# Host layouts, an earlier h and woven tables in the first mixer of a hybrid trunk

## The chip, the cores and the metric

The kernel runs on one core of a Trainium2 chip. Its time is in device microseconds (us), the median of several executions. A profiled execution stands beside it; its span is the time from the first to the last instruction. Engines are named as in the profile: PE (matmuls and transposes), DVE, ACT, POOL (elementwise work) and SP (here a queue that only issues transfers).

## The reference

Two layers over 256 latent tokens and 256 context tokens of width 1024. Layer 0 mixes with a long convolution ("Hyena") on 768 channels beside a state space model ("S5") on 256; layer 1 mixes with a gated linear recurrence; each is followed by a mixture of experts (MoE). The change concerns what leads up to the mixer of layer 0.

```python
def rmsnorm(x, g):
    x32 = x.astype(F32)
    y = x32 * lax.rsqrt(jnp.mean(x32 * x32, axis=-1, keepdims=True) + EPS)
    return (y * g).astype(x.dtype)
...
def s5_discretise(lam_re, lam_im, log_step, b_re, b_im):
    lam = lax.complex(lam_re.astype(F32), lam_im.astype(F32))
    dt = jnp.exp(log_step.astype(F32))[..., None]
    lam_bar = jnp.exp(lam * dt)
    b_bar = ((lam_bar - 1.0) / lam)[..., None] * lax.complex(b_re.astype(F32), b_im.astype(F32))
    return lam_bar, b_bar
...
    p_lat = h_lat @ w_in
    u_lat = s5_in(p_lat)
    st_lf = s5_scan(u_lat, lam_bar[0], b_bar[0], st_cf[:, -1], False)
...
        y = jnp.concatenate([hyena_mix(p[..., :3 * HY_D], filt, conv_w, conv_b, hy_bias),
                             s5_readout(u, st_f, st_b, c_mat, d, glu_w, glu_b)], axis=-1)
        return y.astype(p.dtype) @ w_out
```

Here h is the normed input, scaled and shifted per channel by values made from a conditioning vector (the "modulation"); `w_in` projects it to 2304 channels for the convolution and 256 for the state space.

## The kernel before

`layer0_mixer` works in stages. `boot` loads x and ctx as tokens by channels (`x_sb`), transposes them on PE into `xT` (channels by tokens), squares and sums them (`sq`, `ssq`), makes the reciprocal root (`rs`, spread over partitions by `dg`), and multiplies (`nm`). Four modulation tiles `mod(0)` to `mod(3)`, 8 matmuls of a 2 MB weight tile each with 4 transposes behind them, give scale and shift; `modulate(0)` and `modulate(1)` turn halves of `nm` into h. h is kept as a high part `h_0` (ACT) and a remainder `h_1`: DVE computes scale and shift once more, then subtracts the high part.

Between these steps `boot` works off small generators: `s5_powers` (powers and phasors of the state space, `pw`, `ph`; the phasors on POOL through `tE`, `tF`, `tG`, `st`), `s5_inout` (tables `wB`, `C`, from `brow` and `crow` by transposes), `filter_net` (a two-layer net of the convolution's filters, `hdn`, `kf`, `r`).

A projection block (class `Channels`) is 128 output channels. Its weights are split into a high part `whi` (ACT) and a remainder `wlo` (POOL; for the very first block DVE); 24 matmuls of 512 columns follow, three for each of 8 slices of h (`mm3`: whi on h_0, whi on h_1, wlo on h_0). Blocks and further modulation tiles (`Mods`) form a list `fill`, and `drive(main, fill)` writes a main generator's work with as much fill between its steps as the step names for a gap. The order within each engine is fixed when the program is built.

The main generators after `boot` are `s5_mixer`, `s5_glu` (its matmuls read `gw`) and the convolutions. `s5_mixer` first runs the two blocks for its own channels (`uT`), then four quarters. A quarter is: `U,Gm` matmuls, copies `pq` on ACT, a chain of about 8 us on DVE (`tA`, `rot`, `sc`, `prev`), beside it small matmuls `Hm,wB` and `C,wB` whose result `KX` is spread by 8 transfers into `Km`, and at the end matmuls on `Km` and `prev`. Quarters meet the next through `Gm`; a transpose chain (`y`, `YT`) ends them. A convolution unit runs `zv` matmuls, DVE products, `yy` matmuls and again, six units in all.

2 MB weight tiles come through a ring of three buffers (`Feed.load`, on SP, in order); a tile is loaded when the one in its buffer has been read for the last time.

Of the kernel before, what the change touches and what calls it, by code (L numbers as in the profile page):

```python
# [237 lines left out]
def boot(E, o, feed, hT, hdn2):  # L238

    a, V, SY = E.a, E.V, E.SY
    pers = E.pers
    spec = [
        ('c', a['c'].rearrange("o (k p) -> (o k) p", p=P)),
        ('cc', a['c_ctx'].rearrange("(k p) -> k p", p=P)),
        ('n1', a['norm1_g'].rearrange("l (k p) -> (l k) p", p=P)),
        ('mb', a['mod_b'].rearrange("l (k p) -> (l k) p", p=P)),
        ('cw', a['hy_conv_w'].rearrange("o w (k p) -> (o w k) p", p=P)),
        ('cb', a['hy_conv_b'].rearrange("o (k p) -> (o k) p", p=P)),  # L250
        ('hb', a['hy_bias'].rearrange("o r (k p) -> (o r k) p", p=P)),
        ('glb', a['s5_glu_b'].rearrange("o (k p) -> (o k) p", p=P)),
        ('n2', a['norm2_g'].rearrange("l (k p) -> (l k) p", p=P)),
        ('cg', a['c_norm_g'].rearrange("o (k p) -> (o k) p", p=P)),
        ('lb', a['c_lower_bounds'].rearrange("d l (k p) -> (d l k) p", p=P)),
    ]
# [25 lines left out]
    def rows(gi):  # L282
        rt = bp.tile([P, P], F32, name=f"rows{gi}")
        for nm, ap, r0, r in groups[gi]:
            SY.dma_start(rt[r0:r0 + r, :], ap)
            E.prm[nm] = pt[:, gi, r0:r0 + r]
        return rt[:r0 + r], gi

    def columns(rt, gi):
        n = rt.shape[0]  # L290
        b = E.bank("s5")
        E.tr(b[:, :n], rt)
        E.copy(pt[:, gi, :n], b[:, :n])
# [3 lines left out]
    r0 = rows(0)
    x_sb = bp.tile([P, 4, D], F32, tag="x", name="x_sb")
    SY.dma_start(x_sb[:, 0:2, :], a['x'][0].rearrange("(j p) d -> p j d", p=P))
    SY.dma_start(x_sb[:, 2:4, :], a['ctx'][0].rearrange("(j p) d -> p j d", p=P))  # L300
    pows = s5_powers(E, o, E.tp)
    next(pows)
    feed.load()
    flt = filter_net(E, hdn2, bp)
    next(flt)
    feed.load()
    inout = s5_inout(E, o, E.tp)
    next(inout)
    feed.load()

    columns(*r0)
# [5 lines left out]
    late = []  # L317

    def sums(k, sq):
        for j in range(4):  # L320
            E.mm(ssq[32 * j:32 * j + 32, :n4], E.ones[:, :32], sq[:, j * n4:(j + 1) * n4], k == 0, k == KD - 1)

    def mod(q):
        with E.first():
            cols = mod_tile(E, 0, q, feed.ready['m', 0, q], later=True)
        feed.load()

        def finish():
            with E.first():
                cols()  # L330
        return finish
# [16 lines left out]
    with E.tc.manual_schedule(engines={E.TE.engine, E.S.engine}):
        for k in range(KD):
            b = E.bank("s5")  # L350
            for j in range(4):
                E.tr(b[:, j * P:(j + 1) * P], x_sb[:, j, k * P:(k + 1) * P])
            sq = E.mod.tile([P, 512], F32, tag="ms", name="sq", bufs=2)
            if k % 2:
                E.copy(E.xT[:, k, :], b)
            else:
                E.act(E.xT[:, k, :], b, AF.Copy)
            E.act(sq, b, AF.Square)
            late.append((k, sq))
            if k:  # L360
                sums(*late.pop(0))
            steps(pows, 3)
        sums(*late.pop())
# [1 line left out]
        mean_sq(E, ssq, 4, D)
        for _ in rms_g(E, 4, E.bank("s5")):
            steps(pows, 1)
        steps(inout, 1)
        rb = spread(E, 4, bp, "dg", E.bank("s5"))
        cols()  # L370
        nm = bp.tile([P, KD, T], F32, tag="x", name="nm")
        for k in range(KD):
            E.tt(nm[:, k], E.xT[:, k], rb, MUL)
            steps(pows, 2)
        cols = mod(1)
        steps(flt, 2)
        run(pows)
        cols()
        steps(flt, 7)
        cols = mod(2)  # L380
        later = [rows(q) for q in range(1, len(groups))]
        run(flt)
        cols()
        steps(inout, 2)
        with E.first():
            modulate(0)
        cols = mod(3)
        cols()
        wux = feed.ready['ux']
        ws = [split_w(E, wux[:, :, m * P:m * P + P], 0, KD, E.G if m else E.V) for m in range(2)]  # L390
        with E.first():
            modulate(1)
        run(inout)
        T0 = s5_quarter_tables(E, o, 0, E.hp, E.tq)
        next(T0)
        for x in later:
            columns(*x)
    return T0, ws

# [159 lines left out]
def filter_net(E, hdn2, fl):  # L559

    a, SY = E.a, E.SY
    zt = fl.tile([33, 256], F32, name="zt")
    SY.dma_start(zt, a['k_z'])
    fw1 = fl.tile([33, 64], F32, name="fw1")
    SY.dma_start(fw1, a['hy_fw1'][0])
    fw2 = fl.tile([64, 64], F32, name="fw2")
    SY.dma_start(fw2, a['hy_fw2'][0])
    fr = fl.tile([4, 64], F32, name="fr")
    for i, nm in enumerate(('hy_fb1', 'hy_ff1', 'hy_fb2', 'hy_ff2')):
        SY.dma_start(fr[i:i + 1, :], a[nm])  # L570
    yield
    b = E.bank("s5")
    E.tr(b[:64, :4], fr)
    fp = fl.tile([64, 4], F32, name="fp")
    E.copy(fp, b[:64, :4])
    yield
    cur = zt
# [104 lines left out]
def s5_powers(E, o, tp):  # L682
# [16 lines left out]
    yield  # L699
    E.copy(r4[:, 2], bcast(lst, 2, 64))  # L700
    b = E.bank("s5")
    for i in range(3):
        E.tr(b[:, i * 16:(i + 1) * 16], rows[:, i, :])
    lam = tp.tile([P, 3, 16], F32, name="lam")
    E.copy(lam.rearrange("p i g -> p (i g)"), b[:, :48])
# [1487 lines left out]
```

## Time and profile before

| | us |
|---|---|
| median of 3 runs (1487.02 to 1487.53) | 1487.36 |
| profiled execution | 1486.51 |
| its span | 1484.7 |
| PE busy | 1285.4 |
| DVE busy | 809.5 |
| POOL busy | 400.0 |
| ACT busy | 387.5 |

The mean granted clock of TensorE is 0.932 of full speed. What lies outside the span is 1.8 us. Layer 0's mixer takes about the first 530 us.

### The profile page before, as it was taken

What the parts mean: (1) busy time and instruction counts of PE and PEld (TensorE: products, weight loads), DVE (VectorE), ACT (ScalarE), POOL (GpSimd) and SP (SyncE); (2) the same over time, 40 slices, a digit from 0 to 9 for tenths busy, and PEclk for the clock granted to TensorE, in tenths of its full rate; (3) what the DMA queues carried; (4) which work ended last, traced back from release to release, by engine and by line L of the source; (5) the groups of instructions that cost most, each with busy time, mean ns of one, the idle gap of its engine ahead of it and who ended that gap; (6) DMA issues with size and microseconds to landing.
All of it is one profiled execution on the core that took longest, in us unless ns stands there. A gap on an engine that the chain in (4) does not pass through costs nothing. (4 is left out here: it accounts for less than half of the span.)

```text
span 1484.7 us, 18755 instructions
## 1 busy us (share of the span) xinstructions
PE 1285.4 (87%) x7093; PEld 826.7 (56%) x7093; DVE 809.5 (55%) x1785; ACT 387.5 (26%) x655; POOL 400.0 (27%) x326
## 2 busy tenths in 40 slices
PE   6499999898886769999999498979798969999995
PEld 4266766575665443444444277878778733444443
DVE  5856554766666453344335685665656553343443
ACT  2233433132232321111111443333333312121211
POOL 2733431334554321111100452323231221111101
PEclk9699999899988779999999698999999979999998
DMA  8415673145121389999994111211213189999970
GB/s 298 181 57 183 225 259 142 57 144 218 42 91 79 117 340 416 393 388 384 383 385 175 43 62 53 78 64 59 84 60 122 65 339 395 418 419 420 419 314 31
DMA packets 55747, 311.91 MB, mean 210 GB/s; under 512 B 14441, under 2 KB 19994, under 8 KB 24282
## 3 DMA queue, kind: packets, MB, share of 16 engines
q1 hardware_dynamic: 50746, 303.72, 52.2%
q0 software_dynamic: 4608, 6.30, 1.3%
q8 instruction: 61, 1.00, 0.3%
q10 hardware_dynamic: 288, 0.52, 0.1%
q14 instruction: 44, 0.36, 0.1%
HBM read 315.76 MB, written 4.19 MB: 215 GB/s over the span
## 5 line engine op out<-in xcount | busy, mean ns | idle before, releaser
L148 PE MATMUL pg_t<-w,Xe 128*64 128x512 f32 x1024 | 228.7, 599 | 0.0
L148 PE MATMUL in_t<-h,whl 128*128 128x512 f32 (+1 forms) x768 | 147.2, 349 | 3.2 <-DVE h L158 2.4
L148 PEld LDWEIGHTS pg_t<-w,Xe 128*64 128x64 f32 x1024 | 71.1, 138 | 135.7 <-issue 131.1
L161 POOL TENSOR_TENSOR whl<-wraw,whl 128x2048 fp32r<-128x2048 f32 x20 | 93.6, 4684 | 175.6 <-ACT whl L155 175.6
L148 PEld LDWEIGHTS in_t<-h,whl 128*128 128x128 f32 x768 | 121.7, 195 | 22.1 <-POOL h L161 3.1
L148 PE MATMUL py_t<-w,hid 128*64 128x512 f32 x512 | 119.1, 606 | 4.2 <-DVE yl L161 3.0
L164 DVE SCALAR_TENSOR_TENSOR sg<-sg,ws,pg_t 128x256 f32<-128x256 f32 x32 | 15.4, 480 | 180.2 <-ACT sg L155 180.2
L1615 POOL MEMSET Xg<- 128x1024 f32 x32 | 30.4, 959 | 295.6 <-PE ga_t L152 295.6
L164 DVE SCALAR_TENSOR_TENSOR xT<-sc_t,mT,xT 128x256 f32<-128x256 f32 x204 | 90.3, 479 | 29.6 <-PE sc_t L148 28.1
L161 POOL TENSOR_TENSOR wlo<-w,whi 128x1024 fp32r<-128x1024 f32 (+3 forms) x51 | 72.0, 1416 | 107.6 <-ACT whi L155 100.7
L148 PE MATMUL sc_t<-OT,yh 128*128 128x512 f32 (+1 forms) x256 | 90.7, 369 | 10.2 <-DVE xT L164 7.6
L148 PE MATMUL in_t<-h,whi 128*128 128x512 f32 x288 | 97.6, 416 | 2.1 <-ACT ms L155 1.4
L148 PE MATMUL sc_t<-OT,yl 128*128 128x512 f32 (+1 forms) x256 | 82.6, 337 | 0.0
L148 PEld LDWEIGHTS sc_t<-OT,yh 128*128 128x128 f32 x256 | 48.0, 188 | 54.2 <-issue 27.9
L148 PEld LDWEIGHTS py_t<-w,hid 128*64 128x64 f32 x512 | 34.1, 138 | 64.8 <-issue 55.9
L155 ACT ACTIVATE yh<-py_t 128x1024 fp32r<-128x1024 f32 (+1 forms) x34 | 33.1, 974 | 121.5 <-PE py_t L148 117.3
L168 DVE TENSOR_SCALAR OT<-ht_t,ksq 128x512 fp32r<-128x512 f32 (+1 forms) x32 | 19.7, 616 | 81.5 <-PE ht_t L148 81.5
L155 ACT ACTIVATE sg<-pg_t 128x256 f32<-128x256 f32 x32 | 12.3, 385 | 195.3 <-PE pg_t L148 195.2
L148 PEld LDWEIGHTS in_t<-h,whi 128*128 128x128 f32 x288 | 51.5, 190 | 17.9 <-issue 5.2
L148 PE MATMUL at_t<-QA,X 128*128 128x128 f32 x224 | 37.5, 318 | 26.9 <-DVE QA L161 26.9
L1670 POOL DMA_INDIRECT Xg<-rows,ix x32 | 32.3, 1010 | 104.9 <-DVE ws L1676 33.4
L148 PE MATMUL in_t<-whl,h 128*128 128x256 f32 x384 | 56.5, 300 | 3.7 <-POOL whl L161 3.7
(442 smaller groups left out, 2446.1 us busy)
## 6 DMA issues: line engine op xcount, KB each, us to landing
w<-in_w_gu_dram SPq DMA_DIRECT2D x128, 1024.0 KB
w<-in_w_dn_dram SPq DMA_DIRECT2D x64, 1024.0 KB
w<-in_w_mod_dram SPq DMA_DIRECT2D x24, 2048.0 KB
wraw<-in_w_in_dram SPq DMA_DIRECT2D x20, 1024.0 KB
w<-in_w_in_dram SPq DMA_DIRECT2D x5, 2048.0 KB
w<-in_w_out_dram SPq DMA_DIRECT2D x2, 2048.0 KB
cwo<-in_w_out_dram SPq DMA_DIRECT2D x2, 2048.0 KB
rows<-hh SPq DMA_DIRECT2D x6, 512.0 KB
```

What stands on the lines that cost most here:

```text
L148: self.TE.matmul(o, l, r, start=st, stop=sp)
L155: self.S.activation(o, i, f, **k)
L161: (e or self.V).tensor_tensor(o, x, y, op=op)
L164: self.V.scalar_tensor_tensor(o, x, s, y, op0=op0, op1=op1)
L168: (e or self.V).tensor_scalar(o, x, s1, None, op0=op0)
L1615: E.G.memset(X, 0.0)
L1670: E.G.indirect_dma_start(X, None, rows, bass.IndirectOffsetOnAxis(ix[:, pi:pi + 1], 0), bounds_check=n - 1, oob_is_err=False)
```

## The change

The host lays out x transposed, all parameter vectors as columns, and the state space's lam, B, C and D as the tables want them: the transposes in `boot` and most of its small transfers go. `boot` keeps only the norm, the modulation tiles (in the order 0, 2, 1, 3, so that the first half of h needs two of them) and `modulate`, in which ACT now scales and shifts in place, DVE casts the high part, and DVE and POOL subtract by turns. The tables become a main generator `tables`, driven with fill, and their phasors move from POOL to DVE. The two blocks for `uT` become `Inputs` at the head of the fill; the order of blocks changes from 2 `x2`, 4 `vx4`, 4 `x2` to 2 `Inputs`, 6 `x2`, 4 `vx4`. The transfers into `Km` are issued by ACT and not by SP.

```diff
+    SY.dma_start(pt, a['params'])
+    for k in range(0, KD, 2):
+        SY.dma_start(E.xT[:, k:k + 2], a['xT'][:, k:k + 2])
...
-                E.act(hT[0][:, k, sl], t[:, sl], AF.Identity, scale=A[:, r, k:k + 1], bias=mT[:, r, k:k + 1])
-                E.ts(t[:, sl], t[:, sl], A[:, r, k:k + 1], MUL, mT[:, r, k:k + 1], ADD)
-            E.tt(hT[1][:, k], t, hT[0][:, k].bitcast(F32), SUB, E.G if k % 4 == 1 else E.V)
+                E.act(t[:, sl], t[:, sl], AF.Identity, scale=A[:, r, k:k + 1], bias=mT[:, r, k:k + 1])
+            E.copy(hT[0][:, k], t)
+            E.tt(hT[1][:, k], t, hT[0][:, k].bitcast(F32), SUB, E.G if k % 2 else E.V)
...
-        cmul(E, (st[:, 0], st[:, 1]), (ph[:, 0, :, h], ph[:, 1, :, h]), (ph[:, 0, :, h], ph[:, 1, :, h]), (tG[:, 0], tG[:, 1]), G)
-        cmul(E, (ph[:, 0, :, n:2 * n], ph[:, 1, :, n:2 * n]), (ph[:, 0, :, 0:n], ph[:, 1, :, 0:n]),
-             (bcast(st[:, 0], 2, n), bcast(st[:, 1], 2, n)), (tE[:, :, :n], tF[:, :, :n]), G)
+        yield from cmul_g(E, (st[:, 0], st[:, 1]), (ph[:, 0, :, h], ph[:, 1, :, h]), (ph[:, 0, :, h], ph[:, 1, :, h]), (tG[:, 0], tG[:, 1]))
+        yield from cmul_g(E, (ph[:, 0, :, n:2 * n], ph[:, 1, :, n:2 * n]), (ph[:, 0, :, 0:n], ph[:, 1, :, 0:n]),
+             (bcast(st[:, 0], 2, n), bcast(st[:, 1], 2, n)), (tE[:, :, :n], tF[:, :, :n]))
...
-        E.SY.dma_start(Km[16 * i:16 * i + 16], KX[:, :, (7 - i) * 16:(7 - i) * 16 + P])
+        E.S.dma_start(Km[16 * i:16 * i + 16], KX[:, :, (7 - i) * 16:(7 - i) * 16 + P])
...
+class Inputs(Channels):
+
+
+    def after(self):
+        self.E.act(self.y(), self.b, AF.Copy)
...
-        for q in range(4):
+        for q in (0, 2, 1, 3):
             mw(0, q)
...
+        for m in range(2):
+            jobs.append(Inputs(E, feed, 'ux', m * P, 0, hT, lambda m=m: o.uT[:, m]))
         x2('ux', 256, 4)
         x2('ux', 384, 5, True)
+        block('x2')
+        for u in range(4):
+            x2('x2', u * P, u, u == 3)
         block('vx4')
         vx('vx4', 4)
         vx('vx4', 5)
-        block('x2')
-        for u in range(4):
-            x2('x2', u * P, u, u == 3)
-            mod()
+        mod(4)
...
+        def tables():
+            for _ in weave(s5_powers(E, o, tp), filter_net(E, o.net, hdn2, tp)):
+                yield 0.5
+            for _ in s5_inout(E, o, tp):
+                yield 1.0
+            next(tabs)
+            yield 2.0
+
+        drive(tables(), fill)
```

What ACT does from the first modulation tile to the first weight split was, in the program before (`ms` evacuates a modulation tile, `h_0_87` is the high part of h, each x8 is one half of it):

```order
L155 ACTIVATE ms<-in_t 128x512 x2
L155 ACTIVATE hdn_632<-r 64x256
L155 ACTIVATE hdn_80<-r 64x256
L155 ACTIVATE B<-s_t 128x16x16
L155 ACTIVATE C<-s_t 128x256 x2
L155 ACTIVATE h_0_87<-nm,mT_60,A 128x256 x8
L155 ACTIVATE ms<-in_t 128x512
L155 ACTIVATE whi<-w 128x1024 x2
L155 ACTIVATE h_0_87<-nm,mT_60,A 128x256 x8
```

and is now, at the same place:

```order
L172 ACTIVATE ms<-in_t 128x512 x2
L172 ACTIVATE nm<-nm,mT_60,A 128x256 x8
L172 ACTIVATE ms<-in_t 128x512
L172 ACTIVATE C<-C 128x256
L172 ACTIVATE hdn_467<-r 64x256
L172 ACTIVATE hdn_80<-r 64x256
L172 ACTIVATE ms<-in_t 128x512
L172 ACTIVATE nm<-nm,mT_60,A 128x256 x8
L172 ACTIVATE whi<-w 128x1024 x3
```

The first half of h has moved ahead of the filter net, the last `ms` behind it, and the first `whi` behind the second half of h.

POOL, from its first work in the mixer (`h_1_88` is the remainder of h; `ux`, `uy`, `Hm` are tables of the state space's first quarters), now reads:

```order
L178 TENSOR_TENSOR h_1_88<-nm,h_0_87 128x512 x3
L178 TENSOR_TENSOR wlo<-w,whi 128x1024
L178 TENSOR_TENSOR h_1_88<-nm,h_0_87 128x512
L178 TENSOR_TENSOR wlo<-w,whi 128x1024
L178 TENSOR_TENSOR ux<-C,PH 128x512
L178 TENSOR_TENSOR uy<-C,PH 128x512
L175 COPY r_1274<-e_99 128x256
L178 TENSOR_TENSOR Hm<-ux,uy 128x512
L863 MEMSET r_1274 128x4
```

The phasor work (`tG`, `tE`, `tF`, `st`, `ph`) that stood here is gone to DVE, the first block's `wlo` has come from DVE, and ten table operations, of which the last five rows are the first, stand ahead of the third block's `wlo`.

On PE, from the first quarter's `U,Gm` to its end, the program before put 47 projection matmuls (`in_t<-h`) and one modulation tile (`in_t<-w,sc`) beside the quarter's own; it ended so:

```order
L148 MATMUL in_t<-h_0_87,wlo 128x512
L148 MATMUL in_t<-h_0_87,whi 128x512
L148 MATMUL in_t<-h_1_88,whi 128x512
L148 MATMUL s_t<-U,Km 128x64
L148 MATMUL s_t<-prev,Hm 128x64 x2
```

The same stretch is now, whole but for repeats of the quarter's own rows ahead of these:

```order
L165 MATMUL s_t<-Hm,wB 16x112 x4
L165 MATMUL s_t<-C,wB 16x16 x2
L165 MATMUL s_t<-Hm,wB 16x112 x2
L165 MATMUL in_t<-w,sc 32x512 x8
L169 MATMUL tr_t<-ksq,ms 128x128 x4
L165 MATMUL in_t<-h_0_87,whi 128x512
L165 MATMUL s_t<-U,Km 128x64
L165 MATMUL s_t<-prev,Hm 128x64 x2
```

One projection matmul and two modulation tiles are left there. Ahead of the first `U,Gm` stand 288 projection matmuls (84 before). Between `U,Gm` and `prev` of the four quarters there were 47, 48, 52 and 48, and there are 1, 25, 27 and 33. From the first `U,Gm` to the `gw` matmuls there are 120, where there were 273; up to the `gw` matmuls 408 in all, where there were 357, with 8 modulation matmuls more. Up to the third unit's end the counts are equal again.

## Rows read from the trace of the kernel before

**Rows 1.** Windows: us; busy per engine (instructions), granted clock, DMA share, GB/s.
```profile
60.00:70.00 10.00, 1.99 (x5) 0.75 (x3) 10.00 (x10) 0.77 (x1) 8.25 (x6) 0.50 0.18 79
80.00:260.00 180.00, 172.89 (x1100) 123.23 (x1098) 93.73 (x174) 61.87 (x104) 63.31 (x41) 1.00 0.48 179
260.00:450.00 190.00, 167.00 (x773) 118.36 (x773) 130.11 (x271) 48.08 (x90) 80.72 (x60) 0.91 0.32 117
530.00:760.00 230.00, 215.22 (x1018) 101.43 (x1020) 90.10 (x225) 34.47 (x55) 26.18 (x27) 0.97 0.98 391
```

**Rows 2.** Timeline of PE from 70 to 82: start, length, work, wait before it.
```profile
71.50 0.80 PE L148 MATMUL s_t<-h,wlo 128*128 128x512 f32 x1 [9.26 <-DVE wlo L161]
...
81.52 0.71 PE L148 MATMUL in_t<-h,whi 128*128 128x512 f32 x2
```

**Rows 3.** Timeline of ACT, second half of h.
```profile
72.23 4.05 ACT L155 ACTIVATE h<-nm,mT,A 128x256 fp32r<-128x256 f32 x8 [11.47 <-DVE A L164]
```

**Rows 4.** Timeline of DVE from 56 to 80.
```profile
61.31 4.89 DVE L170 TENSOR_SCALAR nm<-nm,A,mT 128x256 f32<-128x256 f32 x4
...
68.87 0.40 DVE L170 TENSOR_SCALAR nm<-nm,A,mT 128x256 f32<-128x256 f32 x1
...
70.24 1.21 DVE L161 TENSOR_TENSOR wlo<-w,whi 128x1024 fp32r<-128x1024 f32 x1
```

**Rows 5.** Groups by line and shape, PE, 0 to 60: busy, mean ns, idle before.
```profile
L152 PE MATMUL s_t<-ksq,x_sb 128*128 128x128 f32 x32 | 7.8, 381 | 5.2 <-DMA x_sb<-in_x_dram 3.3 <-DMA x_sb<-in_ctx_dram 2.0
```

**Rows 6.** Timeline of PE, end of the token sums.
```profile
22.53 0.43 PE L148 MATMUL in_t<-sq,ones 128*32 128x128 f32 x8 [1.08 <-ACT sq L155]
```

**Rows 7.** Timeline of DVE: small table operations, nm, filter net.
```profile
24.19 0.17 DVE L161 TENSOR_TENSOR tA<-pw 128x16 f32<-128x16 f32 x1
24.27 0.17 DVE L161 TENSOR_TENSOR tB<-pw 128x16 f32<-128x16 f32 x1
...
33.53 1.87 DVE L161 TENSOR_TENSOR nm<-xT,s_t 128x512 f32<-128x512 f32 x3
...
42.10 1.18 DVE L164 SCALAR_TENSOR_TENSOR r<-kf,r 64x256 f32<-64x256 f32 x2
```

**Rows 8.** Groups by line and shape, POOL, 20 to 80.
```profile
L161 POOL TENSOR_TENSOR uy<-C,PH 128x512 f32<-128x512 f32 x3 | 3.6, 1191 | 0.0
L161 POOL TENSOR_TENSOR wlo<-w,whi 128x1024 fp32r<-128x1024 f32 x1 | 2.4, 2383 | 0.0
```

**Rows 9.** Timeline of PE from 100 to 240, a quarter's two ends and the glu.
```profile
101.28 2.00 PE L148 MATMUL s_t<-U,Gm 128*128 128x64 f32 x16
...
120.81 0.61 PE L148 MATMUL s_t<-prev,Hm 128*128 128x64 f32 x4
...
232.28 7.03 PE L148 MATMUL s_t<-ycat,gw 128*128 128x512 f32 x16
```

**Rows 10.** Timeline of DVE in that quarter, first and last of its chain.
```profile
104.60 0.69 DVE L161 TENSOR_TENSOR tA<-pq,ph 128x512 f32<-128x512 f32 x1 [5.02 <-ACT pq L155]
...
112.13 1.85 DVE L161 TENSOR_TENSOR prev<-tA,tB 64x256 f32<-64x256 f32 x6
```

**Rows 11.** Timeline of SP's queue in that quarter.
```profile
111.99 5.30 SPq L874 DMA_DIRECT2D Km<-KX  x8
```

**Rows 12.** Timeline of PE in the second convolution unit.
```profile
305.44 0.62 PE L148 MATMUL in_t<-h,whi 128*128 128x512 f32 x2
305.89 0.39 PE L148 MATMUL in_t<-h,wlo 128*128 128x512 f32 x1
306.12 1.89 PE L148 MATMUL pd_t<-yy,dft 128*128 128x256 f32 x8
...
311.48 1.89 PE L148 MATMUL pd_t<-zv,dft 128*128 128x256 f32 x8
```

**Rows 13.** Timeline of DVE there: what those matmuls read.
```profile
300.45 1.28 DVE L161 TENSOR_TENSOR yy<-Z 128x512 f32<-128x512 f32 x2
...
308.22 0.68 DVE L161 TENSOR_TENSOR zv<-pd_t,zx 128x512 f32<-128x512 f32 x1
```

More of the change, by code (lines that the diff above doesn't have):

```diff
@@ L89, with param_columns @@
 NW = (12, 13)
+def param_columns(a):
+    return [(nm, a[src].size // P) for nm, src in PARAMS] + [('fp', 4)]
 def layouts(a):
@@ L274, in boot @@
     V.memset(E.ones, 1.0)
-    E.prm = {}
+    E.prm, c = {}, 0
+    for nm, n in E.pcols:
+        E.prm[nm] = pt[:, c:c + n]
+        c += n
     E.xT = pers.tile([P, KD, T], F32, name="xT")
@@ L280, in boot @@
     bp = E.bp
[L282 to L293, printed above, removed]
-    SY.dma_start(ksq, a['k_sq'])
[L297 to L311, printed above, removed]
+    SY.dma_start(pt, a['params'])
+    for k in range(0, KD, 2):
+        SY.dma_start(E.xT[:, k:k + 2], a['xT'][:, k:k + 2])
+    SY.dma_start(ksq, a['k_sq'])
+    SY.dma_start(o.lam, a['s5_lam'])
+    for _ in range(3):
+        feed.load()
+    zt = E.tp.tile([33, 256], F32, name="zt")
+    SY.dma_start(zt, a['k_z'])
+    fw1 = E.tp.tile([33, 64], F32, name="fw1")
+    SY.dma_start(fw1, a['hy_fw1'][0])
+    fw2 = E.tp.tile([64, 64], F32, name="fw2")
+    SY.dma_start(fw2, a['hy_fw2'][0])
+    o.net = zt, fw1, fw2
+    SY.dma_start(o.B, a['s5_b'])
+    SY.dma_start(o.C, a['s5_c'])
+    SY.dma_start(o.dcol, a['s5_dcol'])
     E.act(E.sc[:, :, 0], E.prm['c'], AF.Silu)
@@ L316, in boot @@
     n4 = T // 4
[L317 to L331, printed above, removed]
     A = bp.tile([P, 2, KD], F32, name="A")
@@ L335, in boot, with mod @@
     g = E.prm['n1'][:, 0:8]
+    nm = bp.tile([P, KD, T], F32, name="nm")
+    def mod(q):
+        cols = mod_tile(E, 0, q, feed.ready['m', 0, q], later=True)
+        feed.load()
+        return cols
     def modulate(h):
@@ L348, in boot @@
     with E.tc.manual_schedule(engines={E.TE.engine, E.S.engine}):
         for k in range(KD):
[L350 to L352 removed]
             sq = E.mod.tile([P, 512], F32, tag="ms", name="sq", bufs=2)
             if k % 2:
[L355 removed]
+                E.tt(sq, E.xT[:, k], E.xT[:, k], MUL)
             else:
[L357 to L358 removed]
@@ L359, in boot @@
[L359 to L363, printed above, removed]
-        cols = mod(0)
[L365 to L371, printed above, removed]
+                E.act(sq, E.xT[:, k], AF.Square)
+            for j in range(4):
+                E.mm(ssq[32 * j:32 * j + 32, :n4], E.ones[:, :32], sq[:, j * n4:(j + 1) * n4], k == 0, k == KD - 1)
@@ L372, in boot @@
+        mean_sq(E, ssq, 4, D)
+        rms(E, 4, E.bank("s5"))
+        rb = spread(E, 4, bp, "dg", E.bank("s5"))
+        cols = mod(0)
         for k in range(KD):
             E.tt(nm[:, k], E.xT[:, k], rb, MUL)
[L374 to L377, printed above, removed]
         cols()
[L379 to L398, printed above, removed]
+        for q in (2, 1, 3):
+            mod(q)()
+            if q > 1:
+                modulate(q - 2)
 def mod_tile(E, l, q, w=None, tr="tr", later=False):
@@ L556, in reduce_angle, with filter_net @@
     yield
[L559 to L577, printed above, removed]
+def filter_net(E, net, hdn2, fl):
+    cur, fw1, fw2 = net
+    fp = E.prm['fp'][:64]
     for i, w in enumerate((fw1, fw2)):
@@ L698, in s5_powers @@
     V.memset(ph[:, 1, :, 0:1], 0.0)
[L699 to L705, printed above, removed]
+    lam = o.lam
     yield
@@ L1385, in layer0_mixer @@
         between, jobs = jobs, between
-        with E.pool("boot", 1) as E.bp, E.pool("s5a", 1, "right") as E.tp:
-            tabs, ws = boot(E, o, feed, hT, hdn2)
+        s5a = ExitStack()
+        tp = E.tp = s5a.enter_context(E.pool("s5a", 1, "right"))
+        o.lam = tp.tile([P, 3, 16], F32, name="lam")
+        o.B = tp.tile([P, 2, 16, 16], F32, name="B")
+        with E.pool("boot", 1) as E.bp:
+            boot(E, o, feed, hT)
         pp.append(l0.enter_context(E.pool("pc", 2)))
@@ L2135, with kernel @@
 @with_exitstack
-def kernel(ctx: ExitStack, tc: tile.TileContext, a, out, dbg=None, stop=None):
+def kernel(ctx: ExitStack, tc: tile.TileContext, a, out, pcols, dbg=None, stop=None):
     E = Env(ctx, tc, a, out, dbg, stop)
     E.pers = ctx.enter_context(E.pool("pers", 1))
+    E.pcols = pcols
     E.dram = ctx.enter_context(tc.tile_pool(name="dram", bufs=1, space=bass.MemoryType.DRAM))
@@ L2189 @@
     with tile.TileContext(nc, **TCARGS) as tc:
-        kernel(tc, aps, out)
+        kernel(tc, aps, out, param_columns(inputs))
     r = _run(nc, [arrays], core_ids=[0])
```

101 lines of the change are left out of this document (28 added, 73 removed).

## The prediction

> **What bounds the kernel now.** I read the windows first, since the share of busy time over the whole span mixes stages. From 80 to 260 us PE is busy 172.9 of 180 us at a granted clock of 1.00; from 260 to 450 it is busy 167.0 of 190 [rows 1]. So from 80 on, what PE has to do decides, with 7 us idle in the state space stage and 23 in the convolutions. From 60 to 70 it is the other way about: PE is busy 1.99 us, DVE 10.00. Beyond the mixer, at 530 to 760, PE and the transfers are both full (215.2 of 230; DMA 0.98), and that stage begins when the mixer ends: a shift there is carried one to one to the end.
>
> The timeline of PE says how the first 80 us end. Its first projection block waits 9.26 us for `wlo`, flows from 71.50 and is followed by the second at 81.52 [rows 2]. That `wlo` is DVE's [rows 4], and on DVE it stands behind the scale and shift of h, whose pieces of 0.40 us take 4.89 us for four while POOL is at work. ACT waits 11.47 us for `A` and makes the second half of h from 72.23 to 76.3 [rows 3]. The end of the boot is thus a chain of DVE, ACT and DVE; PE's transposes in it are cover, not length.
>
> **What the change does to the start.** The first projection block is done at about 80.2 us now: the second starts at 81.52 [rows 2], and eight transposes stand between them. After, step by step:
> - x comes transposed. The 32 transposes (7.8 us busy, waits of 5.2 [rows 5]) and the copies behind them go; the token sums end at 22.9 today [rows 6]. The transfers of x are as large as before, so x is there at about 10, and the 32 short matmuls of sums follow within 1.5 us: 11.5. Root and spread lie between that and `nm`, today among table work; without it I take 6 us, a chain of some twenty short steps at 0.2 to 0.4, and `nm` starts at 17.5. Eight of them at 0.62 (three took 1.87 [rows 7]) end at 22.4.
> - DVE has 69 small table operations ahead of the reduction for tile 2. They follow each other by 0.08 to 0.12 (24.19 and 24.27 [rows 7]): 6.8 us, so `A` is there at 30 and ACT has the first half of h at 34 (4.05 for eight, [rows 3]).
> - DVE then does about 90 more ahead of the second `A`: some 70 small ones (6 to 7 us), 14 of the filter net at 0.6 (8.3 [rows 7]: two took 1.18), 4 casts and 2 subtractions, which I put at 0.6 to 0.7 as `nm` (4): 18 us, 48. ACT's second half ends at 51.8, the first `whi` at 52.9, and POOL's `wlo`, 2.38 us [rows 8], at 55.4.
> - PE starts then on 24 matmuls. At full clock one takes 0.23 (305.44 to 306.12 for three [rows 12]); after a boot with little PE work the granted clock is 0.50, the lower of the two levels, 1.2 of 2.4 GHz (60 to 70 in [rows 1]), so 0.46: half at each is 8 us. Done at about 64, **16 us earlier**. Bounds: 10 if the small operations take the full 0.17 us that one shows alone, 20 if the tables hide in waits.
>
> **What it adds to the blocks.** POOL now has ten tables of 1.1 us (1191 ns [rows 8]) ahead of the third block's `wlo`: about 11 us from 58 on, then 2.4, so `wlo` comes at 72, and the second block is done at 69.7: 2.3 us of PE idle. Bounds 0 and 8.5, the latter if POOL's tables stretch as DVE's pieces did at 61.31 [rows 4].
>
> **What it moves: the fill.** Projections do not disappear, they move forward. Ahead of the first `U,Gm` now stand 288 of them, 12 blocks of 5.6 us, with six modulation tiles of 1.9 (eight matmuls of 512 columns at the same 0.235) and the state space's and the evacuations' transposes, for which I take 8 us: 64 + 11 x 5.6 + 11.4 + 8 + 2.3 = **150 us** for that `U,Gm`, where it stands at 101.28 today [rows 9]. A load of 2 MB is 5.4 us at the 391 GB/s of the full stage [rows 1]; the weights freed near 130 bring `vx0` about six loads later, at 160, and since the order has `vx0`'s first matmul ahead of `Km` and `prev` of quarter one, that quarter can't end earlier.
>
> A quarter's own chain, bare: `U,Gm` 2.0, the DVE chain from 104.60 to 114.0 less 1.5 of foreign work [rows 10], with ACT's copy between them, 11 to 12 us. Beside it go the 48 small `KX` matmuls (I take 3 us, behind a modulation tile) and eight transfers into `Km`, 5.30 us to issue [rows 11], which ACT must now issue; with `U,Gm` ahead and their landing behind (no row gives it; between 0 and 3, I take 2) 12 to 15. Today 47 to 52 projections, 11 us, and a modulation tile or two fill this stretch, and the first lasts 19.5 us [rows 9]. After, the fill is 1, 25, 27 and 33: it is the chain that decides. I take `U,Gm` to `U,Gm` as 20, 23 and 19 us, and from the fourth to `gw` 25, without the 27 projections that stood behind the last `prev`: 150 + 87 = 237, against 232.28: **5 us later**. Bounds: 1 us earlier (the three chains that `vx0` does not hold 2 us shorter) and 14 later (each `Km` 2.5 us later, the tail uncovered).
>
> At that point PE has done 51 projections and 8 modulation matmuls more than today: 12.0 + 1.9 = 13.9 us of work that the convolutions no longer hold. Nearly all of it leaves the second unit, where 22 projections stay of 72. What can it give there? DVE has `yy` at 301.7 and PE comes to it at 306.12; `zv` is there at 308.9 and PE comes at 311.48 [rows 12, 13]: 7.0 us in which fill stood in the chain's way. With the second pass of that unit and a little of the third I take **9**; the bounds are 7.0 and the whole 13.9.
>
> **The sum.** The 16 us and the 2.3 are inside the 150; what reaches the end is 5 later at `gw`, 9 given back in the convolutions: 4.0 faster. The profiled execution's 1486.51 becomes 1482.5; it lies 0.85 under the median of 1487.36, so as a median 1483.4. That a measurement of this kernel tells from no change is 0.2%, 3.0 us: the forecast lies just beyond it. Its own range is 1479 to 1487. The transposes and small transfers removed beyond the chain count as nothing, since PE has idle time all through the boot; if the chain there became PE's, they would be worth their 7.8 us.
>
> The row at 61.31 shows DVE at a quarter of its pace while POOL works; the phasors now on DVE leave POOL free until 53, and after it POOL's `wlo` and tables meet DVE's casts, subtractions and `Gt` products. The Trainium skill, SBUF — State Buffer, section "Who interferes with whom", says that a GpSimd instruction reading SBUF and a VectorE instruction with two inputs there, or a tensor_scalar in a two-port mode, shut each other out. By that rule, with which the 4.89 us agree, the moved phasors ease the boot and the third block pays. By it alone, with no cover, the sum would be that of the last rival below.
>
> **Rivals.**
> - *The state space runs bare (slower).* Between the first `U,Gm` and `gw` PE has 120 projections in place of 273, so it waits for DVE's and `Km`'s chain in every quarter. For it: the counts, and that ACT, which issues `Km`, also waits there for copies. Against: 25 to 33 projections remain in three of four quarters. The point is 9 us later at `gw`; at 14 later the net is +5: 1492.
> - *PE bounds all through (faster).* If the quarters take no longer than their work, `gw` comes about 1 us earlier and the convolutions give 10 to 14: 1472 to 1476. For it: 172.9 of 180 busy now. Against: that share is made by the very fill that is moved away.
> - *The gain evaporates (no difference).* The convolutions have 23 us idle for DVE, and fill done earlier may only lengthen that; 5 later and 5 to 7 back is 1486 to 1487. The same comes if h gains only 10 us, from slow small operations on DVE or from the second half's `ms`, which stands behind both sines of the filter net on ACT.
> - *Contention.* POOL's ten tables stretched against DVE's products, four of which lost 3.3 us at 61.31, would delay the third block by up to 6 us more (the bound of 8.5 less 2.3): net +2, 1489.
>
> **How the numbers follow.** Forecast 0.43, bare state space 0.18, PE-bound 0.13, evaporated 0.20, contention 0.06. Of the forecast's share, 0.36 lies beyond 3.0 us; with 0.13 that makes 0.49 faster. Same gets 0.07 of the forecast, the 0.20 and 0.02: 0.29 in all. Slower is left with 0.22. The range reaches to near the ends of the first two rivals, 1474 to 1493; cases of both signs hold most of the chance, so the likeliest one's own range, above, stands beside it.
>
> **What the new profile would show.** Right: the first projection matmuls flow from about 55 and the third block waits about 2 us for POOL's `wlo`; the first `U,Gm` at about 150; between it and `gw` PE idle of 10 to 20 us behind `Km`, `prev` or `vx0`; `gw` at 235 to 240; the second convolution unit about 9 us shorter than now. Wrong: a start beyond 60, idle over 25 us between `U,Gm` and `gw`, or a second unit as long as before.

## The result and the profile after

The changed kernel takes 1506.6 us (1504.6 to 1507.0, 4 runs) against 1487.2 before: 1.0129 of it, with a 95% interval of 1.0111 to 1.0146. It is slower by about 19 us where 4.0 faster had been forecast, and lies outside the range of 1474 to 1493. Its profiled execution has a span of 1502.8 us, 18.1 more than before.

The mixer can be cut at three places that both traces have: the end of the first projection block, the first `U,Gm`, and `gw`; the twelfth `zv` group closes it. These are windows (us; busy per engine and instructions; granted clock, DMA share, GB/s) of the kernel before, for its state space stage, its convolutions, and the whole from first block to twelfth `zv`:

```profile
101.30:232.30 131.00, 127.09 (x887) 92.66 (x887) 73.19 (x130) 46.73 (x82) 50.60 (x34) 1.00 0.56 208
232.30:471.40 239.10, 211.18 (x978) 147.26 (x977) 155.72 (x327) 62.31 (x115) 93.73 (x71) 0.92 0.31 115
80.40:471.40 391.00, 356.89 (x1962) 254.31 (x1961) 236.96 (x467) 115.23 (x206) 152.66 (x109) 0.95 0.39 142
```

and of the changed kernel, the stretch that answers to 60 to 70 in [rows 1], then the way to the first `U,Gm`, and the same three:

```profile
60.00:70.00 10.00, 6.40 (x15) 5.02 (x16) 9.90 (x5) 0.00 (x0) 10.00 (x6) 0.51 0.00 0
71.70:160.50 88.80, 84.70 (x441) 61.45 (x439) 19.51 (x36) 26.28 (x40) 31.97 (x19) 0.96 0.46 177
160.50:268.00 107.50, 88.91 (x623) 66.49 (x621) 55.97 (x107) 31.74 (x58) 41.06 (x30) 0.86 0.41 148
268.00:488.20 220.20, 195.02 (x904) 136.38 (x904) 150.66 (x322) 57.21 (x109) 87.08 (x68) 0.92 0.30 109
71.70:488.20 416.50, 368.63 (x1964) 264.33 (x1963) 226.14 (x463) 115.23 (x207) 160.12 (x117) 0.91 0.36 133
```

The first block is through 8.7 us earlier (71.7 for 80.4). From there the same number of matmuls (1964 and 1962 records) takes 416.5 us where it took 391.0: 25.5 more. Of these, 13.8 are PE standing still (47.9 us for 34.1) and 11.7 are the same matmuls running slower (368.6 us busy for 356.9), at a mean granted clock of 0.91 for 0.95. The loss sits in the state space stage: 18.6 us idle in 107.5 at a clock of 0.86, where there were 3.9 in 131.0 at 1.00. The convolutions are 18.9 us shorter, since part of the fill that stood in them is done already.

The timeline of PE shows the places (start, length, work, wait before it):

```profile
57.13 1.22 PE L165 MATMUL in_t<-h,whi 128*128 128x512 f32 x2 [7.42 <-ACT whi L172]
63.60 0.80 PE L165 MATMUL in_t<-h,wlo 128*128 128x512 f32 x1 [5.25 <-POOL wlo L178]
81.33 0.79 PE L165 MATMUL in_t<-h,wlo 128*128 128x512 f32 x1 [3.67 <-POOL wlo L178]
...
160.53 2.00 PE L165 MATMUL s_t<-U,Gm 128*128 128x64 f32 x16
177.25 0.80 PE L165 MATMUL in_t<-h,whi 128*128 128x512 f32 x1 [4.98 <-ACT whi L172]
183.59 0.66 PE L165 MATMUL s_t<-U,Km 128*128 128x64 f32 x2 [5.55 <-DMA w<-in_w_mod_dram]
184.05 1.06 PE L165 MATMUL s_t<-prev,Hm 128*128 128x64 f32 x4
190.88 2.75 PE L165 MATMUL s_t<-U,Gm 128*128 128x64 f32 x16
...
267.99 8.70 PE L165 MATMUL s_t<-ycat,gw 128*128 128x512 f32 x16
```

Block one waits for POOL's `wlo` until 63.6 [rows 2: 71.5], the third block again. In the first quarter PE waits twice for about 5 us. Four `prev` matmuls take 1.06 after that wait and took 0.61 in [rows 9], and `U,Gm` 2.75 for 2.00: the granted clock has fallen to the lower of its two levels (0.50 from 183.6 to 190.2). `gw` comes at 268.0 [rows 9: 232.28].

The way to that start: DVE's `nm`, ACT's second half of h, POOL's first work behind it (answering to [rows 8]), and two of the operations that DVE does meanwhile:

```profile
18.89 4.87 DVE L178 TENSOR_TENSOR nm<-xT,s_t 128x512 f32<-128x512 f32 x8 [0.85 <-PE s_t L165]
52.09 4.04 ACT L172 ACTIVATE nm<-nm,mT,A 128x256 f32<-128x256 f32 x8 [3.55 <-DVE A L181]
55.44 5.36 POOL L178 TENSOR_TENSOR h<-nm,h 128x512 fp32r<-128x512 f32 x1 [16.46 <-DVE h L175]
60.72 2.82 POOL L178 TENSOR_TENSOR wlo<-w,whi 128x1024 fp32r<-128x1024 f32 x1
57.75 0.68 DVE L178 TENSOR_TENSOR tx<-wB,PG 128x512 f32<-128x512 f32 x1
61.38 2.71 DVE L178 TENSOR_TENSOR tx<-wB,PG 128x512 f32<-128x512 f32 x1
```

ACT and its queue in the first quarter, answering to [rows 11], then DVE's last step there, and under it what the view of the tile `Km` says of all 32 transfers:

```profile
168.54 0.71 ACTq L764 DMA_DIRECT2D Km<-KX  x1
170.98 5.11 ACTq L764 DMA_DIRECT2D Km<-KX  x5
176.14 2.00 ACT L172 ACTIVATE whi<-w 128x1024 fp32r<-128x1024 f32 x2 [4.58 <-DMA Km<-KX]
168.78 1.88 DVE L178 TENSOR_TENSOR prev<-tA,tB 64x256 f32<-64x256 f32 x6
```

```profile
DMA to landing us min/median/max: 2.0/2.8/7.7
```

`vx0`'s `whi` stands behind the issue of `Km` on ACT, and the matmuls on `Km` start 7.5 us after the last issue, while two weight tiles move. (PE's row at 183.59 names a weight tile that landed at the same time; `prev` had been ready since 170.7.)

### The profile page after: what moved, and what is told of

It reads as the page before. It is cut to its first block, busy times and chain, and to the rows that moved or that the text cites. A ratio compares the mean times of both kernels' runs of the same rounds, so it can differ in the third digit from the quotient of the medians.

```text
span 1502.8 us, 18336 instructions
## 1 busy us (share of the span) xinstructions
PE 1279.9 (85%) x6921; PEld 824.2 (55%) x6921; DVE 797.3 (53%) x1827; ACT 381.9 (25%) x644; POOL 386.9 (26%) x269
## 5 line engine op out<-in xcount | busy, mean ns | idle before, releaser
L165 PEld LDWEIGHTS pg_t<-w,Xe 128*64 128x64 f32 x1024 | 71.1, 138 | 135.9 <-issue 131.3
L165 PE MATMUL in_t<-h,whi 128*128 128x512 f32 x320 | 109.6, 423 | 14.8 <-ACT whi L172 12.4
L181 DVE SCALAR_TENSOR_TENSOR sg<-sg,ws,pg_t 128x256 f32<-128x256 f32 x32 | 15.4, 481 | 182.0 <-ACT sg L172 182.0
L1528 POOL MEMSET Xg<- 128x1024 f32 x32 | 30.4, 958 | 296.3 <-PE ga_t L169 296.3
L181 DVE SCALAR_TENSOR_TENSOR xT<-sc_t,mT,xT 128x256 f32<-128x256 f32 x204 | 90.3, 479 | 29.6 <-PE sc_t L165 28.1
L165 PEld LDWEIGHTS in_t<-h,whi 128*128 128x128 f32 x320 | 63.0, 203 | 33.0 <-ACT whi L172 13.0
L165 PE MATMUL in_t<-h,wlo 128*128 128x512 f32 x160 | 67.6, 423 | 8.9 <-POOL wlo L178 8.9
L165 PEld LDWEIGHTS py_t<-w,hid 128*64 128x64 f32 x512 | 34.1, 138 | 64.8 <-issue 55.9
L172 ACT ACTIVATE whi<-w 128x1024 fp32r<-128x1024 f32 (+3 forms) x52 | 34.3, 664 | 110.0 <-PE in_t L165 85.1
```

Source lines behind the costliest of these rows:

```text
L165: self.TE.matmul(o, l, r, start=st, stop=sp)
L172: self.S.activation(o, i, f, **k)
L181: self.V.scalar_tensor_tensor(o, x, s, y, op0=op0, op1=op1)
L1528: E.G.memset(X, 0.0)
```

## The experiments

Theory A: the state space stage runs bare, since its fill was moved ahead of it (the first rival). Theory B or K: `Km` is at fault, by its queue or by its landing. Theory C: the start is late, by POOL. Twelve kernels were run; all times are medians, ratios are to the kernel before on the same chip. One thing must be kept in mind: the order on PE is fixed when a kernel is built, and an edit of `Km`'s transfers, of the gaps or of the blocks moves projections from one quarter to another. How many lie between `U,Gm` and `prev` in each quarter was counted in every trace; the counts stand in a table at the end of this section.

**Km back on SP.**

```diff
-        E.S.dma_start(Km[16 * i:16 * i + 16], KX[:, :, (7 - i) * 16:(7 - i) * 16 + P])
+        E.SY.dma_start(Km[16 * i:16 * i + 16], KX[:, :, (7 - i) * 16:(7 - i) * 16 + P])
```

> The changed kernel with the transfers into Km issued by SP again, as before the change. Theory A (the state space stage runs bare because its fill was moved ahead of it): the quarters still wait for their own chain, 1503 to 1508 us. Theory B (Km, issued by ACT, lands late behind weight loads and holds ACT up): the 10.5 us that PE waits for vx0's whi and for Km in the first quarter go, and some of the later quarters' waits, 1492 to 1498 us.

1516.4 us (1.0193, 1.0176 to 1.0210): 10 slower than the change, against both expectations. PE's timeline, SP's queue and the state space stage:

```profile
247.36 0.66 PE L165 MATMUL s_t<-U,Km 128*128 128x64 f32 x2 [7.19 <-DMA Km<-KX]
```

```profile
206.36 5.06 SPq L764 DMA_DIRECT2D Km<-KX  x8
211.52 0.53 SPq L191 DMA_DIRECT2D w<-in_w_mod_dram  x1
240.12 28.17 SPq L764 DMA_DIRECT2D Km<-KX  x16
```

```profile
159.30:284.30 125.00, 97.93 (x622) 73.03 (x621) 58.72 (x107) 31.94 (x59) 41.42 (x30) 0.77 0.35 127
```

SP issues nothing from 212 until `KX` is there at 240, but that holds up no fill: the last weight tile ahead of `gw` went out at 211.5, and the next stands behind `gw`, as it does in the change. What differs is PE's order. Between `U,Gm` and `prev` there are now 56, 32, 0 and 0 projections, where the change has 1, 25, 27 and 33. The first two quarters are longer for it (38.6 and 33.8 us for 30.4 and 28.1), and the last two, with no projection at all, are no shorter (22.6 and 30.0 for 21.3 and 27.7). PE idles 27.1 us in the stage, at a clock of 0.77. So this run does not compare the two queues at one order; it shows how long a bare quarter is.

**Fewer blocks ahead, order as changed.**

```diff
-            for _ in weave(s5_powers(E, o, tp), filter_net(E, o.net, hdn2, tp)):
-                yield 0.5
+            for i, _ in enumerate(weave(s5_powers(E, o, tp), filter_net(E, o.net, hdn2, tp))):
+                yield 0.5 if i % 3 == 0 else 0
```

> The changed kernel with two of three gaps between the tables' steps closed, so that 228 projection matmuls stand ahead of the first U,Gm in place of 288, and 39 (not 1) between it and prev. Theory A: the first quarter no longer stalls, gw comes 10 to 15 us earlier while the convolutions keep up to 14 us more work, net 3 to 10 us faster, 1496 to 1503 us. Theory B: Km is as late as before, 1503 to 1508 us.

1518.4 us (1.0208, 1.0189 to 1.0227), 12 slower than the change: the expectation of A failed. PE's timeline in the second quarter:

```profile
185.00 1.92 PE L165 MATMUL in_t<-w,sc 128*32 128x512 f32 x16 [1.87 <-DMA w<-in_w_mod_dram]
190.16 1.12 PE L169 MATMUL tr_t<-ksq,ms 128*128 128x128 f32 x4 [3.24 <-ACT ms L172]
192.89 0.66 PE L165 MATMUL s_t<-U,Km 128*128 128x64 f32 x2 [1.62 <-DMA Km<-KX]
```

What came into that quarter was five modulation tiles in a row and no projection. Each needs a 2 MB load for 1.9 us of PE, so PE waits for them too. Fill that is bound by its own loads covers little. Over the stage PE idles 26.0 us of 153.0, at a clock of 0.82.

**All of h_1 on DVE.**

```diff
-            E.tt(hT[1][:, k], t, hT[0][:, k].bitcast(F32), SUB, E.G if k % 2 else E.V)
+            E.tt(hT[1][:, k], t, hT[0][:, k].bitcast(F32), SUB, E.V)
```

> The changed kernel with all subtractions of h_1 on DVE, so that POOL's first work is the first block's wlo. Theory C (late start: POOL's h_1 of 5.36 us stands ahead of wlo): the first wlo is done at about 59.5 in place of 63.5 and everything behind shifts by 3 to 5 us, 1501 to 1504 us. Theories A and B: a start that comes earlier is taken up by the weight loads and the bare chain, under 2 us, 1504 to 1508 us.

1500.4 us (1.0084, 1.0066 to 1.0101), 6 faster than the change: the direction of C (its range began at 1501), and the shift reaches the end. PE's order behind the start is that of the change. But the first `wlo` came little earlier; PE and POOL:

```profile
62.81 0.80 PE L165 MATMUL in_t<-h,wlo 128*128 128x512 f32 x1 [6.68 <-POOL wlo L178]
```

```profile
54.94 10.59 POOL L178 TENSOR_TENSOR wlo<-w,whi 128x1024 fp32r<-128x1024 f32 x2 [54.49 <-ACT whi L172]
```

Two `wlo` of 2.38 each [rows 8] took 10.59 beside DVE's subtractions, phasors and products: taking work off POOL does not help while DVE holds it up. The gain came from the blocks behind (second and third `wlo`), and the first `U,Gm` stood at 154.9 for 160.5. That gain is kept although the stage is as bare as in the change.

**The kernel before with Km on ACT.**

```diff
-        E.SY.dma_start(Km[16 * i:16 * i + 16], KX[:, :, (7 - i) * 16:(7 - i) * 16 + P])
+        E.S.dma_start(Km[16 * i:16 * i + 16], KX[:, :, (7 - i) * 16:(7 - i) * 16 + P])
```

> The kernel before with the transfers into Km issued by ACT, nothing else. Theory A: its quarters are bound by PE's fill, so a Km that lands some us later is hidden, 1485 to 1490 us. Theory B: ACT is held up by the issue and Km lands behind the loads in every quarter, 1495 us or more.

1502.4 us (1.0110, 1.0083 to 1.0138): 15 slower, as B had it; `Km` was not hidden there. PE and ACT's queue in the first quarter, and the stage:

```profile
124.50 0.66 PE L148 MATMUL s_t<-U,Km 128*128 128x64 f32 x2 [4.75 <-issue]
124.95 1.06 PE L148 MATMUL s_t<-prev,Hm 128*128 128x64 f32 x4
```

```profile
112.48 4.47 ACTq L874 DMA_DIRECT2D Km<-KX  x7
```

```profile
100.60:248.70 148.10, 132.68 (x861) 97.61 (x860) 71.90 (x128) 44.24 (x78) 48.68 (x33) 0.91 0.49 181
```

ACT issues for some 5 us, and with it the work that PE's fill needs (`ms`, `pc`, `whi`) starts later; PE waits 4.75, 2.8 and 3.7 us ahead of `U,Km` in three quarters, and the next `prev` rows take 1.06 for 0.61. PE's order has moved as well (42, 48, 43 and 30 projections for 47, 48, 52 and 48), so the 15 us are not the queue's alone.

**The old fill.** The order of blocks of the kernel before, and one gap in six.

```diff
-        block('x2')
-        for u in range(4):
-            x2('x2', u * P, u, u == 3)
         block('vx4')
         vx('vx4', 4)
         vx('vx4', 5)
-        mod(4)
+        block('x2')
+        for u in range(4):
+            x2('x2', u * P, u, u == 3)
+            mod()
...
-                yield 0.5
+                yield 0.5 if i % 6 == 0 else 0
```

> The changed kernel with the order of blocks of the kernel before (4 vx4 ahead of 4 x2, the modulation tiles spread among them) and one gap in six between the tables' steps left open: 144 projection matmuls ahead of the first U,Gm, and 36, 42, 36 and 36 between U,Gm and prev. Theory A (the state space stage runs bare because its fill was moved ahead of it): each quarter is covered again and the earlier h is kept, gw at 225 to 240, 1478 to 1490 us. Theory K (Km's transfers are late in any order, and each stall is followed by a low granted clock): 1498 us or more.

1496.4 us (1.0058, 1.0038 to 1.0077): 10 faster than the change, between the two expectations. Its stage:

```profile
110.30:244.70 134.40, 123.71 (x844) 90.07 (x843) 69.26 (x128) 43.28 (x79) 47.96 (x33) 0.95 0.52 192
```

The projections are back (36, 42, 36 and 36), PE idles 10.7 us, and `gw` comes at 244.7.

**The old fill and Km on SP** (both edits).

> As the last, with the transfers into Km issued by SP. If issue by ACT costs as much here as it did in the kernel before (15 us), this is 10 to 15 us faster than the last, 1470 to 1480 us if theory A is right there. If SP's queue is the slower one, as it was in the changed kernel, it is 5 to 10 us slower than the last.

1480.5 us (0.9950, 0.9934 to 0.9966): 15.9 faster than the last and faster than the kernel before. Its stage, its convolutions and the whole from the first block:

```profile
112.35:243.60 131.25, 126.84 (x873) 91.03 (x872) 68.74 (x130) 47.15 (x83) 51.24 (x34) 0.99 0.57 209
243.60:464.20 220.60, 193.49 (x910) 135.04 (x909) 152.58 (x321) 56.65 (x107) 89.61 (x69) 0.93 0.30 108
70.00:464.20 394.20, 357.49 (x1963) 255.05 (x1962) 230.06 (x464) 115.49 (x207) 162.22 (x118) 0.95 0.38 141
```

The first block is through at 70.0, 10.4 us earlier than before the change, and everything behind it takes 394.2 us, where it took 391.0. With its stage covered (4.4 us idle in 131.25, clock 0.99), 7 of these 10.4 us reach the end. With SP the build put more projections into the quarters than in the last run (48, 52, 46 and 36 for 36, 42, 36 and 36), so here too the 15.9 us belong to queue and order together.

**Without Km**, in the change and in the kernel before.

```diff
-    for i in range(8):
-        E.S.dma_start(Km[16 * i:16 * i + 16], KX[:, :, (7 - i) * 16:(7 - i) * 16 + P])
+    E.G.memset(Km, 0.0)
```

> The changed kernel without the transfers into Km: Km is set to zero by POOL, so the direct term of the state space is left out. Theory K: the waits for Km and for the buffer that KX holds go, and with them the low clock behind them: gw 15 to 25 us earlier, 1485 to 1494 us. Theory A: the chain on DVE is as long as Km's and the fill is still missing, gw 3 to 6 us earlier, 1500 to 1504 us.

> The kernel before with the same left out. Under both theories Km is hidden behind PE's fill there: 1483 to 1488 us.

1503.5 us (1.0111, 1.0090 to 1.0133) for the change, 3 faster, which the intervals don't separate from it; 1482.8 (0.9971, 0.9954 to 0.9988) for the kernel before, 4.5 faster, just below its expectation, so `Km` was not wholly hidden there. The change's stage and whole without `Km`, then PE's longest wait in that stage and the 5 us behind it:

```profile
160.90:253.20 92.30, 84.16 (x579) 59.26 (x578) 57.07 (x105) 30.38 (x56) 37.16 (x31) 0.85 0.36 139
72.20:486.40 414.20, 371.27 (x1963) 265.14 (x1963) 231.17 (x463) 115.24 (x207) 160.20 (x120) 0.91 0.35 132
```

```profile
180.14 0.55 PE L165 MATMUL s_t<-Hm,wB 64*16 64x112 f32 x2 [1.91 <-POOL Hm L178]
```

```profile
180.00:185.00 5.00, 4.86 (x47) 2.69 (x47) 4.96 (x4) 2.33 (x5) 4.92 (x4) 0.50 0.03 11
```

`gw` comes 15 us earlier, as K had it, but with 369 projections ahead of it in place of 408, some 9 us of work, and the convolutions get longer by 13.0. The end obeys A. PE idles only 8.1 us in the stage and never waits longer than 1.91, and yet the clock is as low as with `Km` (0.85): the low clock does not hang on the long waits for `Km`. Take `Km` away, and little is won. Since PE's order moved too (0, 10, 11 and 13), the run does not say what `Km`'s waits cost by themselves.

**The order alone**, all gaps open, Km on ACT (the first part of the edit of the old fill).

> The changed kernel with the block order of the kernel before (4 vx4 ahead of 4 x2, the modulation tiles spread among them), all gaps between the tables' steps open, Km by ACT: 240 projection matmuls stand ahead of the first U,Gm, which comes near 150, and 72, 36 and 34 are left for the first three quarters, 0 behind the last. If it is the order that matters (the modulation tiles no longer bunched behind their loads), 1496 to 1500 us, as with the old fill; if it is how many stand ahead, 1502 to 1508 us.

1504.5 us (1.0112, 1.0090 to 1.0134): not told apart from the change. With 240 projections ahead of the first `U,Gm` the later quarters are bare all the same: in the last PE waits 7.4 us for `Km`. Neither fewer ahead alone (1518.4) nor the order alone helps; together they are worth 10 us, and with SP 26. (The two are not exact halves: one gap in three was left open in the one, 228 projections ahead, and one in six in the other, 144.)

**PE kept busy in the first quarter's wait.** The 32 matmuls added are read by nobody.

```diff
+            if q == 0:
+                for _ in range(32):
+                    E.mm(b, o.hT[1][:, 0, 0:P], o.hT[0][:, 0, :], True, True)
...
+        o.hT = hT
```

> The changed kernel with 32 matmuls of 512 columns more, whose result nobody reads, in the first quarter between KX and the matmuls on Km (7.5 us of work where PE stood idle for 11.7). If PE's low clock behind the wait is a price of its own, the matmuls behind it run at full clock and the kernel is 3 to 8 us faster although it does more: 1498 to 1503 us. If only the wait counts, 1504 to 1510 us.

1520.0 us (1.0209, 1.0179 to 1.0240), outside both expectations. PE's timeline:

```profile
171.06 6.87 PE L165 MATMUL s_t<-h,h 128*128 128x512 f32 x29
184.13 0.66 PE L165 MATMUL s_t<-U,Km 128*128 128x64 f32 x2 [6.19 <-DMA Km<-KX]
```

The work was too short to reach the end of the wait, which stays at 184; it pushed `vx0`'s first projection behind it, and the second quarter took 35.5 us for 28.1. What the low clock costs by itself is not told by this run.

**The start, on the kernel with the old fill and Km on SP**: h_1 and the first two `wlo` on DVE.

```diff
-            E.tt(hT[1][:, k], t, hT[0][:, k].bitcast(F32), SUB, E.G if k % 2 else E.V)
+            E.tt(hT[1][:, k], t, hT[0][:, k].bitcast(F32), SUB, E.V)
...
+    def prep(self):
+        E = self.E
+        self.w = split_w(E, self.feed.ready[self.key][:, :, self.col:self.col + P], 0, KD, E.V)
```

> The kernel with the old fill and Km on SP (1480.5 us), with all subtractions of h_1 and wlo of the first two blocks on DVE, as the kernel before had the first. POOL then has nothing ahead of its ten tables, and these are through before the third block. If the start is bound by POOL's wlo, PE flows from about 58 to 59 in place of 63.3, the 5.2 us wait for the third block's wlo goes, and the low clock behind it: 1470 to 1476 us. If the gain at the start is taken up by the state space's chain, 1478 to 1482 us.

1469.0 us (0.9868, 0.9850 to 0.9887), the fastest of all, a little better than expected. PE, DVE, and the whole from the first block:

```profile
54.31 1.74 PE L165 MATMUL in_t<-h,whi 128*128 128x512 f32 x3 [6.12 <-ACT whi L172]
55.95 0.79 PE L165 MATMUL in_t<-h,wlo 128*128 128x512 f32 x1
```

```profile
54.69 1.21 DVE L178 TENSOR_TENSOR wlo<-w,whi 128x1024 fp32r<-128x1024 f32 x1
```

```profile
63.00:455.80 392.80, 361.41 (x1964) 258.00 (x1963) 234.40 (x468) 115.55 (x207) 163.19 (x117) 0.94 0.38 141
```

DVE makes the first `wlo` in 1.21 us, the block is through at 63.0 (7.0 earlier than with the old fill and Km on SP, 17.4 earlier than before), and the rest again takes 392.8, with PE's order unchanged.

**The phasors on POOL again**, on the same base.

```diff
-        yield from cmul_g(E, (st[:, 0], st[:, 1]), (ph[:, 0, :, h], ph[:, 1, :, h]), (ph[:, 0, :, h], ph[:, 1, :, h]), (tG[:, 0], tG[:, 1]))
+        yield from cmul_g(E, (st[:, 0], st[:, 1]), (ph[:, 0, :, h], ph[:, 1, :, h]), (ph[:, 0, :, h], ph[:, 1, :, h]), (tG[:, 0], tG[:, 1]), E.G)
...
-             (bcast(st[:, 0], 2, n), bcast(st[:, 1], 2, n)), (tE[:, :, :n], tF[:, :, :n]))
+             (bcast(st[:, 0], 2, n), bcast(st[:, 1], 2, n)), (tE[:, :, :n], tF[:, :, :n]), E.G)
```

> The kernel with the old fill and Km on SP, with the phasors on POOL again. If moving them to DVE was worth its while, POOL's wlo comes behind 30 us of phasors and ten tables, PE flows from 70 or later, and the kernel is 5 to 12 us slower than 1480.5: 1485 to 1493 us. If not, 1476 to 1482 us, since DVE is freer.

1491.2 us (1.0022, 1.0011 to 1.0032), 10.7 slower than with them on DVE, as expected. PE:

```profile
80.41 0.79 PE L165 MATMUL in_t<-h,wlo 128*128 128x512 f32 x1 [23.29 <-POOL wlo L178]
```

PE's order is again that of the old fill. The move of the phasors is worth its while as long as POOL makes the first `wlo`; with `wlo` on DVE it was not tried.

**The counts, by quarter.** Idle is the length of the state space stage less PE's busy time in it.

| kernel | projections between `U,Gm` and `prev` | PE idle, of the stage's us | granted clock |
|---|---|---|---|
| before | 47, 48, 52, 48 | 3.9 of 131.0 | 1.00 |
| old fill, Km on SP | 48, 52, 46, 36 | 4.4 of 131.3 | 0.99 |
| old fill, Km on ACT | 36, 42, 36, 36 | 10.7 of 134.4 | 0.95 |
| before, Km on ACT | 42, 48, 43, 30 | 15.4 of 148.1 | 0.91 |
| change | 1, 25, 27, 33 | 18.6 of 107.5 | 0.86 |
| order alone | 72, 36, 34, 0 | 18.7 of 119.6 | 0.86 |
| fewer ahead | 39, 0, 18, 29 | 26.0 of 153.0 | 0.82 |
| change, Km on SP | 56, 32, 0, 0 | 27.1 of 125.0 | 0.77 |

The barer the quarters are left, the more PE idles and the lower its clock. That speaks for theory A, and it fits that SP won with the old fill and lost with the new order. Two things stay open. The change without `Km` (0, 10, 11 and 13 projections) idles only 8.1 us of 92.3, so most of the idle needs `Km`'s chain as well as the missing fill. And what the queue costs at one and the same order no run shows.

## Why the prediction was wrong

- **The start** was forecast 16 us earlier and is 8.7. Up to the second half of h the steps held with a few us of delay (`nm` at 18.9 for 17.5, second half on ACT at 52.1 for 47.8). Then POOL's `h_1`, for which the forecast had no time ahead of `wlo`, took 5.36 us, and `wlo` 2.82: 63.6 for 55.4. The contention that the forecast put at the third block, as the last rival, came at the first. The rule cited (the Trainium skill, SBUF — State Buffer, "Who interferes with whom") fits: DVE ran casts and two-input operations back to back meanwhile, one of them took 2.71 us while POOL's `wlo` ran and 0.68 while POOL's `h_1` was held up, and `wlo` on DVE took 1.21. What the prediction claimed for the 4.89 us at 61.31 [rows 4] is less sure: whether those pieces ran in a two-port mode no row shows. Nor were they at a quarter of their pace; by its own 0.40 us a piece it is a third.
- **The first `U,Gm`** came at 160.5 for 150. The terms of that sum add up to 147.3, not 150; with 147.3 the same working gives about 7 us faster, which is further off still. The rest is the later start and a third block that waited 3.7 us for 2.3 and then ran at a low clock.
- **The state space stage** is the step that failed: "5 us later" at `gw` were 35.7. The quarters took 30.4, 28.1, 21.3 and 27.7 us (to `gw`) for 20, 23, 19 and 25, 107.5 for 87. At the pace that each kind of matmul has in the trace before, those left in the stage come to about 77 us (an estimate from the two traces). So 87 left room for 10 us of idle at full clock. Idle was 18.6, inside the 10 to 20 that the prediction named as a sign of being right. The matmuls took 88.9: the low clock, at nothing in the sum, cost about 12, more than half of the 20.5 missing. Named in the forecast were the landing of `Km` (2 us; it was up to 7.7 while weights moved) and that `vx0` would hold the first quarter. Left out were that the issue holds `whi` on ACT, that PE falls to half clock in a stage like this, and that the transfers and weight loads of a bare stage come together. Its rival, the bare state space, had the sign and the place, but its end, 14 later, was far too small; the bounds were made from chains whose parts were each taken without a wait.
- **The convolutions** gave back 18.9 us, not 9, more than the bound of 13.9. So the second term was too small as well; the rows of one unit had shown 7.0 of it, and which unit gave the rest was not taken apart. 35.7 less 18.9 is 16.8, and with 1.3 behind the mixer it makes the 18.1 between the spans.
- That cover decides, and not one wait, is borne out by the old fill with Km on SP (394.2 us behind the first block, 391.0 before), by the run without `Km`, and by the counts of all runs. The old fill with Km on ACT is still 9 us slower than the kernel before, with 36 to 42 projections in each quarter; a price of the queue itself may lie in that, and is not separated. How the 25.5 us divide into waiting and clock is read from one trace (13.8 and 11.7) and was not separated by a run.
- **Issue by ACT** was costed only as length. The kernels with it are 10 us faster with the change's fill and 15 to 16 slower with the two old ones, each time with another order on PE; the forecast had no term for either.

## What to carry to other kernels

Fill that is moved ahead is not gained: price the stage that it leaves by its bare chain with all its waits, transfers behind weight loads and a lower clock, and keep the fill where the chain is. An earlier start reached the end in both orders (first `U,Gm` 5.7 us earlier and 6 faster in the bare one; first block 10.4 and 17.4 us earlier, 7 and 18 faster than before in the covered one); what ate it in the change was the 25.5 us added behind it. Which queue was the better one for small transfers turned around with the order here, so try it again whenever the order changes, and count what the build has moved before blaming the queue.

## What was not expected of the hardware

- After a PE wait of about 5 us, four matmuls that take 0.61 us took 1.06, and the mean granted clock of the stage was 0.86: the same number of matmuls was 11.7 us longer over the mixer. In the run without `Km` the clock was at 0.50 behind a wait of only 1.91 us.
- A 32 KB transfer took 2.0 us to land at the least, 2.8 at the median and 7.7 at the most, the last while 2 MB weight tiles moved.
- Beside DVE at work, POOL's subtraction of 128x512 took 5.36 us, and two `wlo` 10.59 where one takes 2.38 alone.
- A cast of 128x512 on DVE took 0.41 us (mean of eight in the changed kernel), not the 0.6 to 0.7 that had been taken from `nm`.
